# A decoder step on one core: the second feed-forward layer with Strassen products for all eleven pairs of hidden tiles

## The chip, the cores and the metric

The kernel runs as one launch on one core of a Trainium2 chip. The metric is the device time of that launch in microseconds; smaller is better. Engines are named as in the profile: PE multiplies matrices (PEld loads its stationary operands), DVE is the vector engine, ACT the scalar engine, POOL is GpSimd, SP issues the DMAs.

## The reference, cut to what matters

One inference step of a two-layer decoder trunk over 512 prompt rows and 32 sample rows, all in float32. Layer 0 is a half feed-forward, a gMLP mixer, a second half feed-forward and a gated input embedding; layer 1 has an attention mixer instead. The change touches the second feed-forward of layer 0 and the end of the gMLP in front of it:

```python
h = h + 0.5 * swiglu(rmsnorm(h, ffn1_norm[i]), ffn1_w1[i], ffn1_w3[i], ffn1_w2[i])
xn = rmsnorm(h, mix_norm[i])
mix, v_rows = gmlp_mix(xn, ...)           # ends with (u * s) @ w_out
h = h + mix
h = h + 0.5 * swiglu(rmsnorm(h, ffn2_norm[i]), ffn2_w1[i], ffn2_w3[i], ffn2_w2[i])
...
def swiglu(x, w1, w3, w2):
    return (jax.nn.silu(x @ w1) * (x @ w3)) @ w2
```

The model is 1024 wide, the hidden layer 2816 wide.

## The kernel before

**Data.** The residual stream lies transposed in SBUF: eight tiles `h[c]` of 128 rows (channels) and T = 544 columns (tokens). A float32 product is made of three products of rounded parts: an operand x is split into `hi` (ACT, a cast to fp32r) and `lo` = x - hi (DVE), and PE adds hi·hi, hi·lo and lo·hi. So each weight block of 128x1024 costs one load (512 KB, SP), one ACT cast and one DVE subtraction (`_split`) before PE can use it.

**The gMLP's end.** Eight output tiles, one per `c`, 48 matmuls each (`tile_mm`, `mm`: 8 stationary blocks, 3 parts, columns in two pieces of 256 and 288). After each, DVE adds the result to `h[c]` (L667), and `on_chunk(c)` prepares the next norm: `prep` makes the split of g·h (ACT L297 for hi, DVE L298 for lo; g is the norm's gain), `ssq` squares h (ACT L324) and POOL adds the square to the norm's sum (L326). After c = 1, 3 and 5 `forms` builds, for a pair of tiles, the sums of quarters that the Strassen products need (ACT L307, DVE L311 to L314, and two splits, ACT L285 and DVE L286).

**The feed-forward layer.** The 2816 hidden rows are 11 pairs of two 128-row tiles (of `w1` and `w3` at once). Pair 0 is **plain**: four `tile_mm` with the columns in full, whose first also brings the norm's factor: `rstd` splits the sum of squares, sums it over the partitions with four matmuls (L362), and `rsqrt_steps` makes 1/sqrt of it on ACT and DVE. Pairs 1 to 10 are **Strassen** pairs in Winograd's form: the 256 x 1024 block times 1024 x 544 as seven products (`products`, named "1" to "7") of 24 matmuls with 272 columns, into PSUM tiles A, B and C; four of the seven weight operands are sums of blocks that DVE makes (`_sum`, L184), all seven are split. `evict` combines the products in SBUF, `gate` multiplies by rstd, silu and product. Between the products stand the matmuls of the second matrix (`second`).

**What sets the order.** Weights are a stream of `pieces`; `prepare` at piece u splits to u + 2, makes sums to u + 2 (in the layer u + 3) and loads to u + 4 (u + 6), by `self.ahead`. All 128x1024 blocks come from one pool of 45 buffers, so a load waits until an older block is let go. The gMLP is ordered by a scheduler when the program is built; the layer's steps (`ffn_steps`) keep the order of the code on PE, ACT, DVE and POOL. On the chip each engine takes its instructions in that fixed order.

Of the kernel before, what the change touches and what calls it, by code (L numbers as in the profile page):

```python
# [26 lines left out]
ALU = mybir.AluOpType  # L27
# [27 lines left out]
PLAIN = (2, 1, 1, 1)  # L55

SEVEN = "1562734"

# [36 lines left out]
class Builder:  # L95
# [37 lines left out]
    def set_stream(self):  # L133
        self.chain, self.pending, self.bg, self.pages = None, [], [], {}
        self.aps, self.raws = [], {}
        self.pieces, self.sums, self.split = [], {}, {}
# [12 lines left out]
    def seven(self, aps):  # L149
# [5 lines left out]
        for k, x, op, y in (("5", a21, "+", a22), ("6", (r, "5"), "-", a11), ("7", a11, "-", a21),  # L155
                            ("3", a12, "-", (r, "6"))):
            d[k] = dict(key=(r, k), sum=(x, op, y))
        for v in d.values():
            v.update(n=1024)
# [14 lines left out]

    def _sum(self):
        p = self.pieces[self.p_sum]
        self.p_sum += 1
        if p["sum"] is None:
            return
        a, op, b = p["sum"]  # L180
        get = lambda x: self._raw(x, 1024) if isinstance(x[1], int) else self.sums[x]
        a, b = get(a), get(b)
        t = self.flat(1024)
        self.nc.vector.tensor_tensor(t, a, b, ALU.add if op == "+" else ALU.subtract)  # L184
        self.sums[p["key"]] = t
# [184 lines left out]
    def ffn_slots(self, skip=1):  # L370
# [16 lines left out]
    def ffn_pieces(self, n):  # L387
# [4 lines left out]
        for kind, at, k, part in self.ffn_slots(PLAIN[n]):  # L392
            if kind == "g":
                if at not in d:
                    d[at] = self.seven([i["w13"][n, at - 1, x] for x in range(4)])
# [10 lines left out]
    def ffn(self, h, box, gcol, rstd, on_chunk, plain=1):  # L406
# [30 lines left out]
        assert self.chain is None  # L437
        for j, a, g in first:
            todo[a].extend(([None] * 3 if j == 0 else []) + self.gate(hid, rstd, j, a, g))
        with self.tc.manual_schedule(engines={eng.PE, eng.Activation, eng.DVE, eng.Pool}):  # L440
            self.ffn_steps(h, xf, rstd, hid, todo, plain, on_chunk)
# [23 lines left out]
    def ffn_steps(self, h, xf, rstd, hid, todo, plain, on_chunk):  # L465
# [8 lines left out]
        def products(j, k, part):  # L474
            if k == "1" and j not in tiles:
                tiles[j] = {}
            t = tiles[j]
            if k in "152" and "ABC"["125".index(k)] not in t:
                if k == "2":
                    t["B"] = [self.pb()[:, :HT] for _ in range(2)]  # L480
                else:
                    t["A" if k == "1" else "C"] = self.ps()[:, :, :HT]
            out = t["A" if k in "1674" else "C" if k in "53" else "B"]
            dst = out if k == "2" else [out[:, w] for w in range(2)]
            hi, lo = self.take()
            for kp in range(NKP):
                xh, xl = xf[kp][k]
                for n, (a, b) in enumerate(((hi, xh), (hi, xl), (lo, xh))):
                    for w in range(2):
                        c = slice(512 * w + P * kp, 512 * w + P * kp + P)  # L490
                        nc.tensor.matmul(dst[w], a[:, c], b, start=k in "152" and kp == 0 and n == 0,  # L491
# [3 lines left out]
        def evict(j, k):  # L495
            t = tiles[j]
            if k in "156":
                t["r" + k] = q2(self.tmp())
                nc.scalar.copy(t["r" + k], t["C" if k == "5" else "A"])  # L499
                return  # L500
            if k == "2":
                t["g"] = self.big(), self.big()
            g = t["g"]
# [5 lines left out]
            elif k == "3":  # L509
# [1008 lines left out]
```

## Time and profile before

| | before |
|---|---|
| time, median of 3 runs | 2063.28 us (2062.68 to 2063.79) |
| time of the profiled execution | 2064.12 us |
| its span, first to last instruction | 2062.4 us |
| PE busy | 2042.4 us, 99% of the span |
| DVE busy | 1507.2 us, 73% |
| ACT busy | 950.4 us, 46% |
| POOL busy | 184.2 us, 9% |

Busy shares are averages over the whole span. PE's idle time, not its share, tells where something can be won or lost, and it is read stage by stage from the waits and the timeline. The profiled execution's own time lies 1.7 us above its span and 0.84 us above the median.

### The profile page before, as it was taken

What the parts mean: (1) busy time and instruction counts of PE and PEld (TensorE: products, weight loads), DVE (VectorE), ACT (ScalarE), POOL (GpSimd) and SP (SyncE); (2) the same over time, 40 slices, a digit from 0 to 9 for tenths busy, and PEclk for the clock granted to TensorE, in tenths of its full rate; (3) what the DMA queues carried; (4) which work ended last, traced back from release to release, by engine and by line L of the source; (5) the groups of instructions that cost most, each with busy time, mean ns of one, the idle gap of its engine ahead of it and who ended that gap; (6) DMA issues with size and microseconds to landing.
All of it is one profiled execution on the core that took longest, in us unless ns stands there. A gap on an engine that the chain in (4) does not pass through costs nothing.

```text
span 2062.4 us, 38838 instructions
## 1 busy us (share of the span) xinstructions
PE 2042.4 (99%) x16432; PEld 2012.4 (98%) x16432; DVE 1507.2 (73%) x1861; ACT 950.4 (46%) x1421; POOL 184.2 (9%) x222
## 2 busy tenths in 40 slices
PE   8999999999999999999999999999999999999999
PEld 8999999999999999999999999999987999999999
DVE  7877777556687778776688777786476888777773
ACT  7534344423554344454456343534365754344451
POOL 0000000410100000043060000001141200000020
PEclk9999999999999999999999999999999999999999
DMA  5233234212223222432374323314669222222431
GB/s 185 84 110 107 74 109 141 97 44 83 83 92 113 73 105 80 154 99 82 107 255 162 113 85 110 105 69 136 193 204 323 99 99 85 100 103 82 130 97 44
DMA packets 93823, 237.95 MB, mean 115 GB/s; under 512 B 9538, under 2 KB 27490, under 8 KB 93650
## 3 DMA queue, kind: packets, MB, share of 16 engines
q1 hardware_dynamic: 93506, 235.44, 34.1%
q8 instruction: 129, 2.11, 0.4%
q14 instruction: 44, 0.36, 0.1%
q10 hardware_dynamic: 144, 0.04, 0.0%
HBM read 218.95 MB, written 16.49 MB: 114 GB/s over the span
## 4 chain that ended last, share of the span: by engine, by line
PE 92%; DVE 3%; ACT 2%; issue 1%; DMA 1%; POOL 0%; SPq 0%; DVEq 0%; ACTq 0%; POOLq 0%
PE ps L491 33%; PE ps L241 16%; PE ps L247 16%; PE ps L245 16%; PE pb L491 5%; DVE big L199 1%; ACT big L198 1%; PE ps L1272 1%; PE ps L1268 1%; PE ps L1271 1%; ACT big L285 0%; DVE big L184 0%; DVE big L286 0%; PE ps L1223 0%; PE ps L829 0%
## 5 line engine op out<-in xcount | busy, mean ns | idle before, releaser
L491 PE MATMUL ps<-big,big 128*128 128x272 f32 x5616 | 727.7, 288 | 1.8 <-DVE big L508 1.3
L491 PEld LDWEIGHTS ps<-big,big 128*128 128x128 f32 x5616 | 714.2, 188 | 2.4 <-issue 1.6
L199 DVE TENSOR_TENSOR big<-big,big 128x1024 fp32r<-128x1024 f32 (+2 forms) x538 | 591.9, 1103 | 105.5 <-ACT big L198 105.0
L198 ACT CAST big<-big 128x1024 fp32r<-128x1024 f32 (+2 forms) x538 | 488.0, 932 | 267.6 <-DVE big L184 262.8
L241 PE MATMUL ps<-big,big 128*128 128x256 f32 (+1 forms) x2684 | 558.8, 289 | 7.6 <-ACT big L198 7.6
L247 PE MATMUL ps<-big,big 128*128 128x256 f32 x2684 | 554.9, 289 | 1.5 <-DVE big L199 1.5
L245 PE MATMUL ps<-big,big 128*128 128x256 f32 x2684 | 554.0, 287 | 0.0
L241 PEld LDWEIGHTS ps<-big,big 128*128 128x128 f32 x2684 | 430.9, 189 | 11.3 <-ACT big L198 8.5
L247 PEld LDWEIGHTS ps<-big,big 128*128 128x128 f32 x2684 | 429.8, 188 | 3.1 <-DVE big L199 2.7
L245 PEld LDWEIGHTS ps<-big,big 128*128 128x128 f32 x2684 | 432.5, 189 | 0.0
L326 POOL TENSOR_TENSOR st<-st,tmp 128x544 f32<-128x544 f32 (+1 forms) x63 | 87.5, 1388 | 1587.7 <-ACT tmp L324 1587.5
L530 DVE SCALAR_TENSOR_TENSOR big<-ps,big 128x544 f32<-128x544 f32 x160 | 115.6, 723 | 106.5 <-PE ps L247 106.4
L184 DVE TENSOR_TENSOR big<-big,big 128x1024 f32<-128x1024 f32 x156 | 190.2, 1219 | 0.0
L499 ACT COPY tmp<-ps 128x544 f32<-128x544 f32 x117 | 71.7, 613 | 141.2 <-PE ps L491 141.2
L454 ACT ACTIVATE big<-big 128x544 f32<-128x544 f32 x88 | 58.0, 660 | 163.2 <-DVE big L451 162.0
L491 PE MATMUL pb<-big,big 128*128 128x272 f32 x936 | 124.0, 288 | 0.0
L451 DVE TENSOR_TENSOR big<-big,st 128x1088 f32<-128x1088 f32 x88 | 113.4, 1290 | 10.6 <-ACT big L513 8.8
L491 PEld LDWEIGHTS pb<-big,big 128*128 128x128 f32 x936 | 120.2, 188 | 0.0
L286 DVE TENSOR_TENSOR big<-big,big 128x544 fp32r<-128x544 f32 (+1 forms) x112 | 82.1, 739 | 36.4 <-ACT big L285 36.3
L297 ACT ACTIVATE big<-big,gains 128x544 fp32r<-128x544 f32 (+1 forms) x80 | 55.8, 704 | 104.6 <-DVE big L530 64.9
L298 DVE SCALAR_TENSOR_TENSOR big<-big,gains,big 128x544 fp32r<-128x544 f32 (+1 forms) x80 | 65.8, 830 | 25.8 <-ACT big L297 25.8
L285 ACT CAST big<-big 128x544 fp32r<-128x544 f32 (+1 forms) x112 | 71.3, 644 | 17.8 <-DVE big L457 9.0
(208 smaller groups left out, 1430.8 us busy)
## 6 DMA issues: line engine op xcount, KB each, us to landing
big<-in_w SPq DMA_DIRECT2D x156, 512.0 KB
big<-in_w2a SPq DMA_DIRECT2D x64, 512.0 KB
big<-in_w2b SPq DMA_DIRECT2D x32, 384.0 KB
big<-in_w13p SPq DMA_DIRECT2D x16, 512.0 KB
big<-in_win SPq DMA_DIRECT2D x16, 512.0 KB
big<-in_wg SPq DMA_DIRECT2D x16, 512.0 KB
big<-in_ck SPq DMA_DIRECT2D x16, 512.0 KB
big<-in_cv SPq DMA_DIRECT2D x16, 512.0 KB
```

Of the source, the lines that this page charges most:

```text
L184: self.nc.vector.tensor_tensor(t, a, b, ALU.add if op == "+" else ALU.subtract)
L198: self.nc.scalar.copy(hi, src)
L199: self.nc.vector.tensor_tensor(lo, src, hi.bitcast(F32), ALU.subtract)
L241: i = nc.tensor.matmul(out[:, a:b], wh, xh[:, a:b], start=s, stop=False)
L245: nc.tensor.matmul(out[:, a:b], wh, xl[:, a:b], start=False, stop=False)
L247: nc.tensor.matmul(out[:, a:b], wl, xh[:, a:b], start=False, stop=e)
L286: self.nc.vector.tensor_tensor(pair[:, 1, cols], src, pair[:, 0, cols].bitcast(F32), ALU.subtract)
L326: nc.gpsimd.tensor_tensor(acc[:, cols], acc[:, cols], sq, ALU.add)
L451: tt(g, g, rstd.unsqueeze(1).broadcast_to([P, 2, T]), ALU.mult)
L491: nc.tensor.matmul(dst[w], a[:, c], b, start=k in "152" and kp == 0 and n == 0, stop=kp == NKP - 1 and n == 2, skip_group_check=True)
L499: nc.scalar.copy(t["r" + k], t["C" if k == "5" else "A"])
L530: nc.vector.scalar_tensor_tensor(h[c], whole(out), 0.5, h[c], ALU.mult, ALU.add)
```

## The change

The second feed-forward layer has no plain pair any more (`PLAIN[1] = 0`): pair 0 is a Strassen pair too. Its products come in the order "1", "2", "3", "6", "5", "7", and "4" follows behind the first product of pair 1; "3" gets a PSUM tile of its own (D), and `evict` combines in another order. From the third last output tile of the gMLP on, `ahead` is (3, 4, 6), so pair 0's loads, sums and splits begin there, and a sum that needs another makes it on demand (`_operand`). The norm's sum is split before the layer's steps (`rstd_parts`), and the four matmuls and the rsqrt come in front of product "6". The fourth `forms` is made after c = 7. Line numbers shift: L199 is L208 after the change, L184 is L186, L298 is L307, L311 to L314 are L320 to L323, L286 is L295, L358 is L366, L362 is L375, L491 is L513, L667 is L692.

```diff
-PLAIN = (2, 1, 1, 1)
+PLAIN = (2, 0, 1, 1)
+PLAIN_FIRST = "123657"
...
+    def _operand(self, x):
+        if isinstance(x[1], int):
+            return self._raw(x, 1024)
+        if x not in self.sums:
+            a, op, b = self.defs[x]
+            a, b = self._operand(a), self._operand(b)
+            t = self.flat(1024)
+            self.nc.vector.tensor_tensor(t, a, b, ALU.add if op == "+" else ALU.subtract)
+            self.sums[x] = t
+        return self.sums[x]
+
     def _sum(self):
         p = self.pieces[self.p_sum]
         self.p_sum += 1
...
+        if p["sum"]:
+            self._operand(p["key"])
...
-    def rstd(self, acc):
-
+    def rstd_parts(self, acc):
         parts = self.tmp(F32R), self.tmp(F32R)
         self.nc.scalar.copy(parts[0], acc)
         self.nc.vector.tensor_tensor(parts[1], acc, parts[0].bitcast(F32), ALU.subtract)
+        return parts
+
+    def rstd(self, acc, parts=None):
+
+        parts = parts or self.rstd_parts(acc)
         sums = [self.pb()[:, :HT] for _ in range(2)]
...
-            gs = [("g", j, k, None) for k in SEVEN]
+            gs = [("g", j, k, None) for k in (SEVEN if j else PLAIN_FIRST)]
+            if j == 1 and skip == 0:
+                gs.insert(1, ("g", 0, "4", None))
...
+        parts = self.rstd_parts(box["acc"]) if rstd is None else None
...
         def products(j, k, part):
+            nonlocal rstd
+            if rstd is None and k == "6":
+                rstd = self.rstd(None, parts)
...
+            own = "3" if j == 0 else ""
+            fresh = k in "152" + own
...
-            out = t["A" if k in "1674" else "C" if k in "53" else "B"]
+            out = t["A" if k in "1674" else "D" if k in own else "C" if k in "53" else "B"]
...
-            if k in "156":
+            if k in "15" or k == ("6" if j else "3"):
                 t["r" + k] = q2(self.tmp())
-                nc.scalar.copy(t["r" + k], t["C" if k == "5" else "A"])
-                return
+                nc.scalar.copy(t["r" + k], t["C" if k == "5" else "D" if k == "3" else "A"])
+            if j == 0 and k == "6":
+                tt(t["r3"], t["A"], t["r3"], add)
...
-            elif k == "3":
-                tt(g[0][:, :, HT:], t["C"], t["r6"], add)
+            elif k == ("3" if j else "5"):
+                tt(g[0][:, :, HT:], t["C"], t["r6" if j else "r3"], add)
...
         for c in range(NC_):
+            if c == NC_ - 3:
+                self.ahead = (3, 4, 6)
             p = self.tile_mm(m)
...
-        on, nxt = self.next_norm(h, G_FFN2, early={1: 0, 3: 1, 5: 2})
+        on, nxt = self.next_norm(h, G_FFN2, early={1: 0, 3: 1, 5: 2, 7: 3})
...
-        self.ffn(h, box, G_FFN2, None, on)
+        self.ffn(h, box, G_FFN2, None, on, PLAIN[1])
...
-        w13.append(np.stack([_blocks(w1[n][:, 256:]), _blocks(w3[n][:, 256:])], 3).reshape(NPAIR - 1, 4, P, 1024))
+        w13.append(np.stack([_blocks(w1[n]), _blocks(w3[n])], 3).reshape(NPAIR, 4, P, 1024))
```

**DVE at the gMLP's last two output tiles.** Before, from the update of `h[6]` (`big_89`, first row) to the prep of `h[7]`; `big_5922` and `big_5984` are the splits of g·h[6] and g·h[7], the L199 rows are splits of the plain pair's weights:

```order
L667 TENSOR_TENSOR big_89<-ps_5872,big_89 128x544
L286 TENSOR_TENSOR big_5858<-tmp_5856,big_5858 128x544
L199 TENSOR_TENSOR big_5867<-big_5732,big_5866 128x1024
L298 SCALAR_TENSOR_TENSOR big_5922<-big_89,gains,big_5922 128x544
L199 TENSOR_TENSOR big_5929<-big_5794,big_5928 128x1024
L667 TENSOR_TENSOR big_89<-ps_5934,big_89 128x544
L298 SCALAR_TENSOR_TENSOR big_5984<-big_89,gains,big_5984 128x544
```

After the change, from the same update; `big_5872` is the block a12 of pair 0 (the operand of product "2"), the three L186 rows are the sums of "5", "6" and "3", and `big_5934` and `big_5994` are the splits of g·h[6] and g·h[7]:

```order
L692 TENSOR_TENSOR big_89<-ps_5884,big_89 128x544
L295 TENSOR_TENSOR big_5860<-tmp_5858,big_5860 128x544
L692 TENSOR_TENSOR big_89<-ps_5944,big_89 128x544
L208 TENSOR_TENSOR big_5875<-big_5872,big_5874 128x1024
L186 TENSOR_TENSOR big_5878<-big_5868,big_5870 128x1024
L186 TENSOR_TENSOR big_5880<-big_5878,big_5732 128x1024
L186 TENSOR_TENSOR big_5882<-big_5872,big_5880 128x1024
L307 SCALAR_TENSOR_TENSOR big_5934<-big_89,gains,big_5934 128x544
L208 TENSOR_TENSOR big_5941<-big_5882,big_5940 128x1024
L307 SCALAR_TENSOR_TENSOR big_5994<-big_89,gains,big_5994 128x544
```

The split of g·h[6], which stood between the two L667 rows, now stands behind the second one, and behind the split for "2" and the three sums; the split of g·h[7] stands behind the split for "3".

**DVE further on in pair 0.** After the change, from the last row of the fourth `forms`; L366 (one row earlier) was the norm's split, `big_6046`, `big_6078` and `big_6119` are the splits for "6", "5" and "7", L529 reads product "2" out of its two PSUM tiles `pb`, `big_6159` is the first split for pair 1, L352 is the first step of the rsqrt:

```order
L295 TENSOR_TENSOR big_6006<-tmp_6004,big_6006 128x544
L208 TENSOR_TENSOR big_6046<-big_5880,big_6045 128x1024
L208 TENSOR_TENSOR big_6078<-big_5878,big_6077 128x1024
L186 TENSOR_TENSOR big_6081<-big_5732,big_5868 128x1024
L529 TENSOR_TENSOR big_6114<-pb_6049,tmp_6075 128x272
L529 TENSOR_TENSOR big_6114<-pb_6050,tmp_6075 128x272
L208 TENSOR_TENSOR big_6119<-big_6081,big_6118 128x1024
L208 TENSOR_TENSOR big_6159<-big_6083,big_6158 128x1024
L352 SCALAR_TENSOR_TENSOR tmp_6129<-st_6128 128x544
```

Before the change the fourth `forms` stood at the plain pair's end, ACT copied the plain tiles out, and nothing on DVE had to read a `pb` tile ahead of the norm's matmuls; now the two L529 rows do, and stand behind two splits and the sum of "7" (`big_6081`).

**PE where the norm's sum is taken.** Before, in the second tile of the plain pair, whose stationary blocks are `big_5928`; L362 reads the norm's split `tmp_6040` into the tiles `pb`:

```order
L241 MATMUL ps_6075<-big_5570,big_5928 128x256
L241 MATMUL ps_6075<-big_5570,big_5928 128x288
L362 MATMUL pb_6044<-tmp_6040,onesr 128x272
L362 MATMUL pb_6045<-tmp_6040,onesr 128x272
L245 MATMUL ps_6075<-big_5570,big_5928 128x256
```

After the change, behind the last stationary block of product "3" (`ps_6089`) and in front of product "6" (`ps_6020`):

```order
L513 MATMUL ps_6089<-big_5994,big_5940 128x272 x4
L513 MATMUL ps_6089<-big_5994,big_5941 128x272 x2
L375 MATMUL pb_6122<-tmp_6014,onesr 128x272
L375 MATMUL pb_6123<-tmp_6014,onesr 128x272
L375 MATMUL pb_6122<-tmp_6015,onesr 128x272
L375 MATMUL pb_6123<-tmp_6015,onesr 128x272
L513 MATMUL ps_6020<-big_5582,big_6045 128x272 x4
L513 MATMUL ps_6020<-big_5582,big_6046 128x272 x2
```

The four matmuls stood among those of a plain tile, two and two; now they stand together between two products, and take the two `pb` tiles that product "2" has held.

## Rows read from the trace of the kernel before

**Rows 1.** The page's first part: busy time of each engine, its share of the span, and the number of its instructions.

```profile
PE 2042.4 (99%) x16432; PEld 2012.4 (98%) x16432; DVE 1507.2 (73%) x1861; ACT 950.4 (46%) x1421; POOL 184.2 (9%) x222
```

**Rows 2.** Who PE waited for: first over the whole execution (two of its eleven rows: the longest, and the next longest single wait), then from 480 to 620 us, where one wait is all there is. Columns: total us, times, longest us.

```profile
PE ps L241 <- ACT big L198: 7.6, 3, 7.1
...
PE pb L1243 <- DVE tmp L1239: 1.1, 1, 1.1
...
PE ps L491 <- DVE big L508: 0.7, 1, 0.7
```

**Rows 3.** PE's instructions in order of time: start us, length us, engine, line, operation, tiles, count; in brackets the idle time before and what ended it. First the first matmuls of the plain pair, then the norm's four, then the first products of the Strassen pairs.

```profile
540.08 0.41 PE L241 MATMUL ps<-big,big 128*128 128x256 f32 x2
...
547.05 0.41 PE L362 MATMUL pb<-tmp,onesr 128*128 128x272 f32 x2
...
564.48 9.23 PE L491 MATMUL ps<-big,big 128*128 128x272 f32 x72
573.54 3.19 PE L491 MATMUL pb<-big,big 128*128 128x272 f32 x24
576.57 6.19 PE L491 MATMUL ps<-big,big 128*128 128x272 f32 x48
583.48 0.74 PE L491 MATMUL ps<-big,big 128*128 128x272 f32 x4 [0.72 <-DVE big L508]
```

**Rows 4.** DVE's instructions in order of time across the end of the gMLP and the start of the second feed-forward layer, same columns.

```profile
529.87 0.79 DVE L298 SCALAR_TENSOR_TENSOR big<-big,gains,big 128x544 fp32r<-128x544 f32 x1 [0.82 <-ACT big L297]
531.70 0.78 DVE L311 TENSOR_TENSOR tmp<-big 128x544 f32<-128x544 f32 x1 [1.04 <-ACT big L307]
532.51 0.44 DVE L313 TENSOR_TENSOR tmp<-big,tmp 128x272 f32<-128x272 f32 x1
532.99 0.44 DVE L314 TENSOR_TENSOR tmp<-big,tmp 128x272 f32<-128x272 f32 x1
533.35 0.72 DVE L286 TENSOR_TENSOR big<-tmp,big 128x544 fp32r<-128x544 f32 x1
534.30 0.72 DVE L667 TENSOR_TENSOR big<-ps,big 128x544 f32<-128x544 f32 x1 [0.24 <-PE ps L247]
534.94 0.72 DVE L286 TENSOR_TENSOR big<-tmp,big 128x544 fp32r<-128x544 f32 x1
535.58 1.22 DVE L199 TENSOR_TENSOR big<-big,big 128x1024 fp32r<-128x1024 f32 x1
536.71 1.89 DVE L298 SCALAR_TENSOR_TENSOR big<-big,gains,big 128x544 fp32r<-128x544 f32 x1
538.52 1.21 DVE L199 TENSOR_TENSOR big<-big,big 128x1024 fp32r<-128x1024 f32 x1
540.28 0.72 DVE L667 TENSOR_TENSOR big<-ps,big 128x544 f32<-128x544 f32 x1 [0.54 <-PE ps L247]
541.88 0.79 DVE L298 SCALAR_TENSOR_TENSOR big<-big,gains,big 128x544 fp32r<-128x544 f32 x1 [0.88 <-ACT big L297]
543.37 1.61 DVE L199 TENSOR_TENSOR big<-big,big 128x1024 fp32r<-128x1024 f32 x1 [0.70 <-ACT big L198]
...
549.90 0.79 DVE L346 SCALAR_TENSOR_TENSOR tmp<-pb,tmp 128x272 f32<-128x272 f32 x2
550.60 1.22 DVE L199 TENSOR_TENSOR big<-big,big 128x1024 fp32r<-128x1024 f32 x1
551.73 0.72 DVE L347 SCALAR_TENSOR_TENSOR st<-tmp,st 128x544 f32<-128x544 f32 x1
```

**Rows 5.** ACT's instructions after the last tile of the gMLP, same columns.

```profile
541.09 0.75 ACT L297 ACTIVATE big<-big,gains 128x544 fp32r<-128x544 f32 x1 [3.74 <-DVE big L667]
541.75 0.64 ACT L324 ACTIVATE tmp<-big 128x544 f32<-128x544 f32 x1
542.30 1.03 ACT L198 CAST big<-big 128x1024 fp32r<-128x1024 f32 x1
```

**Rows 6.** POOL's last two additions to the norm's sum in the gMLP, same columns.

```profile
535.92 2.09 POOL L326 TENSOR_TENSOR st<-st,tmp 128x544 f32<-128x544 f32 x1 [4.03 <-ACT tmp L324]
542.53 1.36 POOL L326 TENSOR_TENSOR st<-st,tmp 128x544 f32<-128x544 f32 x1 [4.52 <-ACT tmp L324]
```

**Rows 7.** SP's loads around the gMLP's output tiles (start us, length us over the merged issues), and the rate of all DMA from 498 to 520 us in 40 slices of 0.55 us (GB/s).

```profile
510.40 6.30 SPq L165 DMA_DIRECT2D big<-in_w13p  x2
...
GB/s 0 0 0 0 0 82 320 410 142 0 0 0 0 0 0 0 0 0 0 0 0 0 0 30 119 127 387 291 45 0 0 0 0 0 0 141 246 372 194 0
```

**Rows 8.** PE at the start of the program: the first matmul and the idle time before it, matmul pairs at 11.71 and at 13.48 us, and the windows from 8 to 10 and 14 to 16 us (busy us and count of PE, PEld, DVE, ACT, POOL, granted clock, DMA share, GB/s).

```profile
7.12 0.82 PE L241 MATMUL ps<-big,big 128*128 128x256 f32 x2 [7.12 <-ACT big L198]
...
11.71 0.66 PE L241 MATMUL ps<-big,big 128*128 128x256 f32 x2
12.17 0.66 PE L245 MATMUL ps<-big,big 128*128 128x256 f32 x2
...
13.48 0.41 PE L245 MATMUL ps<-big,big 128*128 128x256 f32 x2
13.73 0.42 PE L247 MATMUL ps<-big,big 128*128 128x256 f32 x2
...
8.00:10.00 2.00, 2.00 (x9) 1.69 (x9) 1.99 (x4) 1.41 (x3) 0.00 (x0) 1.00 1.03 402
14.00:16.00 2.00, 2.00 (x19) 2.00 (x18) 1.90 (x3) 2.00 (x5) 0.00 (x0) 1.00 0.61 229
```

More of the change, by code (lines that the diff above doesn't have):

```diff
@@ L135, in set_stream @@
         self.aps, self.raws = [], {}
-        self.pieces, self.sums, self.split = [], {}, {}
+        self.pieces, self.sums, self.split, self.defs = [], {}, {}, {}
         self.p_next = self.p_split = self.p_sum = self.a_load = 0
@@ L157, in seven @@
             d[k] = dict(key=(r, k), sum=(x, op, y))
+            self.defs[r, k] = x, op, y
         for v in d.values():
@@ L177, in _sum @@
         self.p_sum += 1
-        if p["sum"] is None:
-            return
[L180 to L185, printed above, removed]
+        if p["sum"]:
+            self._operand(p["key"])
     def _split(self):
@@ L394, in ffn_pieces @@
                 if at not in d:
-                    d[at] = self.seven([i["w13"][n, at - 1, x] for x in range(4)])
+                    d[at] = self.seven([i["w13"][n, at, x] for x in range(4)])
                 self.pieces.append(d[at][k])
@@ L440, in ffn @@
         with self.tc.manual_schedule(engines={eng.PE, eng.Activation, eng.DVE, eng.Pool}):
-            self.ffn_steps(h, xf, rstd, hid, todo, plain, on_chunk)
+            self.ffn_steps(h, xf, rstd, hid, todo, plain, on_chunk, parts)
         self.ahead = (2, 2, 4)
@@ L463, in gate, with ffn_steps @@
         return [one, two, three, four]
-    def ffn_steps(self, h, xf, rstd, hid, todo, plain, on_chunk):
+    def ffn_steps(self, h, xf, rstd, hid, todo, plain, on_chunk, parts):
         nc = self.nc
@@ L477, in products @@
             t = tiles[j]
-            if k in "152" and "ABC"["125".index(k)] not in t:
+            own = "3" if j == 0 else ""
+            fresh = k in "152" + own
+            if fresh:
                 if k == "2":
@@ L481, in products @@
                 else:
-                    t["A" if k == "1" else "C"] = self.ps()[:, :, :HT]
-            out = t["A" if k in "1674" else "C" if k in "53" else "B"]
+                    t["A" if k == "1" else "C" if k == "5" else "D"] = self.ps()[:, :, :HT]
+            out = t["A" if k in "1674" else "D" if k in own else "C" if k in "53" else "B"]
             dst = out if k == "2" else [out[:, w] for w in range(2)]
@@ L490, in products @@
                         c = slice(512 * w + P * kp, 512 * w + P * kp + P)
-                        nc.tensor.matmul(dst[w], a[:, c], b, start=k in "152" and kp == 0 and n == 0,
+                        nc.tensor.matmul(dst[w], a[:, c], b, start=fresh and kp == 0 and n == 0,
                                          stop=kp == NKP - 1 and n == 2, skip_group_check=True)
@@ L496, in evict @@
             t = tiles[j]
-            if k in "156":
+            if k in "15" or k == ("6" if j else "3"):
                 t["r" + k] = q2(self.tmp())
-                nc.scalar.copy(t["r" + k], t["C" if k == "5" else "A"])
-                return
+                nc.scalar.copy(t["r" + k], t["C" if k == "5" else "D" if k == "3" else "A"])
+            if j == 0 and k == "6":
+                tt(t["r3"], t["A"], t["r3"], add)
             if k == "2":
                 t["g"] = self.big(), self.big()
-            g = t["g"]
+            g = t.get("g")
             if k == "2":
@@ L508, in evict @@
                 tt(g[1][:, :, HT:], t["A"], t["r5"], add)
-            elif k == "3":
-                tt(g[0][:, :, HT:], t["C"], t["r6"], add)
+            elif k == ("3" if j else "5"):
+                tt(g[0][:, :, HT:], t["C"], t["r6" if j else "r3"], add)
                 todo[0].extend(self.gate(hid, rstd, j, 0, g[0]))
-            else:
+            elif k == "4":
                 nc.scalar.copy(g[1][:, :, :HT], t["A"])
```

## The prediction

> **What bounds the kernel now.** First the page's busy times: PE is busy 2042.4 of 2062.4 us [rows 1], so a change is worth what it takes from PE's matmuls and what it puts into or takes from PE's waits. Then PE's waits: the longest is 7.1 us at the program's start, the next longest single one 1.1, and from 480 to 620 us, where the change lies, PE waits once, 0.7 us, for DVE's L508 [rows 2]. Then PE's timeline there: the plain pair's first matmul starts at 540.08, the first Strassen product at 564.48, so the plain pair takes 24.40 us without a gap [rows 3]. DVE has room on average, but across this stretch its timeline shows what it must do between the gMLP's last tile and the layer, and in which order [rows 4]. DVE takes its rows in the order in which they stand, so I set the order after the change against the durations of before.
>
> **Matmuls.** Three products (72 matmuls) take 564.48 to 573.54, 9.06 us, and the fourth 573.54 to 576.57 [rows 3]: 3.02 us per product. Seven are 21.1 us; the norm's four matmuls, as wide as a product's (the first two at 547.05), add 4 x 0.126 = 0.5. Against 24.40: **-2.8 us**.
>
> **More work off PE.** Seven splits instead of four and four sums: seven DVE operations of 128x1024 more, at 1.13 us from start to start (550.60 to 551.73 [rows 4]), 8 us, and three ACT casts at 1.03 [rows 5]. Were they spread over the gMLP's last three tiles they would be hidden. So the question is where they stand, and that the order rows in the section on the change show.
>
> **Stall A, in product "1".** Behind the update of h[6] DVE has one more row, then the update of h[7], which waits for the gMLP's last matmul. Before, DVE did two weight splits and the split of g·h[6] in that time (535.58 to 539.7 [rows 4]); after, it has nothing to do there but wait, since split "2", three sums and the split of g·h[6] all stand behind. The data are not late: the loads are let go by blocks that DVE and PE finish by about 513 (the last by the split that follows 511), and the load issued at 510.40 shows its burst in the slices from 510.7 to 513.4 [rows 7], so the last is there by about 517. SP issues as many loads as before, four blocks of pair 0 in the place of four plain ones, and POOL's queue gets nothing; pair 1's loads are let go by matmuls of the gMLP's last tile and read by DVE only from about 559, so they are no term. From the update's start at 540.28 [rows 4]:
> update 0.64 (its step to the next independent row, 534.30 to 534.94), 540.92; split "2" 1.13, 542.05; sums "5" and "6", each waiting for the one before, 1.22 + 0.05 (the gap from L313 to L314 is 0.03), 543.32 and 544.59; sum "3" 1.13, 545.72; split of g·h[6] 0.79, 546.51.
> Product "1" needs that split for its 21st matmul: 540.08 + 20 x 0.126 = 542.6. ACT's hi of g·h[6] now stands behind the square of h[7] and comes at 541.0 + 0.64 + 0.75 = 542.4 [rows 5], just in time. So PE waits **3.9 us**. POOL's addition of that square starts about 541.8 and falls on the first sum. In the trace such a meeting stretched a DVE operation from 0.79 to 1.89 (536.71 against 541.88, POOL from 535.92) and another from 1.23 to 1.61 (543.37, POOL from 542.53) [rows 4, 6]. The bounds are 0 and 1.1 us; the first case is nearer (POOL comes while DVE is busy and takes its turn), so I take **+1.1**. Products "2" and "3" find their operands in time.
>
> **Stall B, before product "6".** The norm's four matmuls write the two tiles that "2" holds, so they wait for both L529 rows. DVE's chain goes on from 545.72 (without POOL's 1.1, which shifts both stalls' ends alike): split "3" waits for sum "3" and its cast (1.07 from cast start to split start, 542.30 to 543.37 [rows 4, 5]), 546.95; split of g·h[7] 548.1; the fourth forms 549.05 to 552.7 (1.65 to its first L286 by 531.70 to 533.35, then three rows at 0.63, the norm's split among them); split "6" to 554.0; split "5", held by its cast behind ACT's copy of "1", from 554.45; sum "7" 555.6; L529 twice from 556.7 to 557.5 (0.70 for two of 272 columns, 549.90 to 550.60, and its own tail). PE arrives at 546.5 + 0.5 + 2 x 3.02 = 553.05 and waits for the second half until 557.4, some of it behind the first: **4.2 us**; 3.6 without the two cast waits, 4.6 if ACT slips further.
>
> **Stall C, "7" and "4".** With the norm at 557.5, "6" ends near 561.0 and "5" near 564.0. "7" goes into the tile that DVE must have read after "6"; that row stands behind two splits and the rsqrt (0.76 + 0.70 + 0.72, as 549.14 to 552.4 before), and ends near 564.7. "4" needs the readout of "7", behind two splits, two sums and a gate: near 571.9 against PE at 570.7. That is 0.7 + 1.2. The one wait of this kind in the trace is 0.7 [rows 2], so 0.7 is the low bound and 2.0 the high one; I take **1.5**. That one, at 583.48, I take off, **-0.7**: DVE comes to pair 1 without that queue behind it. If it stays, 0.
>
> **Sum.** -2.8 + 3.9 + 1.1 + 4.2 + 1.5 - 0.7 = **+7.2 us**. The profiled execution took 2064.12, its span and 1.7 around it, so it would take 2071.3; the median of before is 0.84 lower, and so is my forecast for the median: **2070.5**. The lowest bounds give -2.8 + 3.9 + 0 + 3.6 + 0.7 - 0.7 = +4.7 (2068.0), the highest -2.8 + 3.9 + 1.1 + 4.6 + 2.0 - 0 = +8.8 (2072.1).
>
> **Rivals.** (1) **The clock falls.** At the program's start, after 7.1 us of idle, pairs of matmuls (544 columns) start 0.46 us apart until about 13 us, then 0.25 apart: the lower level, 1.2 GHz, then 2.4, though the column of the granted clock says 1.00 in both windows [rows 8]. A stall could do the same here. Six microseconds at half speed are 3 us lost. After A they would be taken out of B, where PE waits 4.2 anyway, and the end would not move; after B they would cover C, and cost 3.0 - 1.5: 2072.0. Against it: the trace has no wait between 1.1 and 7.1 us [rows 2] that shows it either way. Chance 0.2. The Trainium skill has this as a rule (TensorE: Matmul & The Clock Gate, Part 1): the array's clock drops to half when PE has been idle for a while and returns only after sustained work, and the trace agrees at the program's start; by the row alone the sum is +7.2, with the rule holding after B +8.7.
> (2) **The stalls are partly covered**: DVE's operations come closer together, POOL does not get in the way, and B shrinks to about 2. Then -2.8 + 3.9 + 2 + 0.7 - 0.7 = +3.1, 2066.4. It decides if L529 is done by about 555.3. Speaking against: the chain has 12 DVE rows behind A and hardly a gap. Chance 0.1, half of it within 0.2%.
> (3) **Faster.** The operations of DVE are done before the update of h[7], in the 5 us of idle that PE's last tile leaves; then A is gone, B begins 5 us earlier and is gone too, C stays small: -2.8 to -1.5, 2060.5 to 2061.8. It decides if the split of g·h[6] is there by 542.6. The order puts it behind the update, so this needs the instructions to run otherwise than they stand. Chance 0.04.
> (4) **No effect**: pair 0 is worth 2.8 us of PE and the stalls happen to be worth as much; within 0.2%, 0.06.
>
> **How the numbers follow.** A measurement of this kernel can tell about 0.2% (4.1 us) from no change. The likeliest case (0.6) gives 2070.5; with rival 1 the slower side by over 0.2% (above 2067.4) holds 0.85, with half of rival 2; within 0.2% 0.11; faster 0.04. The range leaves out rival 3 and the low half of rival 2 and goes above the highest bound for the clock: 2066.8 to 2073.0.
>
> **What would show it.** Right: after about 542.6 PE waits some 4 to 5 us in the first Strassen product for the split of g·h[6] (L307), DVE idle before the update of h[7] from about 536 to 540; a second wait of about 4 us of the norm's matmuls (L375) for L529; one or two of about 1 us behind; 24 matmuls fewer. PE pairs at 0.46 us behind a stall would show rival 1. Wrong: no wait at L513 near 542, or DVE busy on weights from 536 to 540; then the loads or the order are not what I read.

## The result, and the profile after

The changed kernel takes **2069.9 us** (median of 7 runs, 2069.03 to 2070.89) against 2063.3 for the kernel before on the same chip (7 runs): a ratio of 1.0031, 95% interval 1.0021 to 1.0040, so +6.6 us. The profiled execution took 2069.03 with a span of 2067.2 (before: 2064.12 and 2062.4).

In the changed file the lines have moved: L513 holds the products' matmuls, L375 the norm's, L307 the split of a normalized tile, L208 and L207 a weight's split and its cast, L186 the sums, L529, L523 and L531 the read-outs of "2", "6" and "7", L692 the update of h.

The page's first part, as [rows 1]: 24 matmuls fewer, PE busy 0.9 us less, DVE 10.6 us more, and the span 4.8 us longer.

```profile
PE 2041.5 (99%) x16408; PEld 2010.8 (97%) x16408; DVE 1517.8 (73%) x1873; ACT 953.2 (46%) x1424; POOL 186.1 (9%) x222
```

PE's waits from 480 to 640 us, which answer to the last of [rows 2] (total us, times, longest). The single wait of before, 0.7 us for L508, is gone, and four others stand there, 6.9 us together.

```profile
PE ps L513 <- DVE big L307: 4.7, 1, 4.7
PE ps L513 <- DVE big L531: 0.9, 1, 0.9
PE pb L375 <- DVE big L529: 0.8, 1, 0.8
PE ps L513 <- DVE tmp L523: 0.5, 1, 0.5
```

PE's timeline, as [rows 3] (start us, length us, instruction, count, in brackets the idle time before and what ended it). The first matmul of pair 0 starts at 539.62; product "2" of pair 2, which started at 595.57 before, now starts at 602.08.

```profile
539.62 2.89 PE L513 MATMUL ps<-big,big 128*128 128x272 f32 x20
547.23 1.27 PE L513 MATMUL ps<-big,big 128*128 128x272 f32 x4 [4.73 <-DVE big L307]
548.30 5.35 PE L513 MATMUL pb<-big,big 128*128 128x272 f32 x24
553.49 3.15 PE L513 MATMUL ps<-big,big 128*128 128x272 f32 x24
557.43 0.90 PE L375 MATMUL pb<-tmp,onesr 128*128 128x272 f32 x4 [0.79 <-DVE big L529]
558.16 6.16 PE L513 MATMUL ps<-big,big 128*128 128x272 f32 x48
564.81 6.26 PE L513 MATMUL ps<-big,big 128*128 128x272 f32 x48 [0.48 <-DVE tmp L523]
571.94 9.26 PE L513 MATMUL ps<-big,big 128*128 128x272 f32 x72 [0.87 <-DVE big L531]
...
602.08 3.16 PE L513 MATMUL pb<-big,big 128*128 128x272 f32 x24
```

This stretch, from the first matmul of the second feed-forward layer to product "2" of pair 2, is the measure used for every run below: 595.57 - 540.08 = 55.5 us before, 62.5 after, **+7.0**. What lies behind it differs from one profile to another in no relation to the edits (it takes between 1465.1 and 1467.4 us in all the profiles here, 1466.8 before and 1465.1 in the change); with that, and 0.5 us less ahead of it, the span moved by only 4.8. The row to notice is the third: product "2", 24 matmuls, took 548.30 to 553.49, 5.19 us, where a product takes 3.02 [rows 3]. The windows say why (busy us and count of PE, PEld, DVE, ACT, POOL, then the granted clock, DMA share, GB/s):

```profile
541.00:547.00 6.00, 1.51 (x11) 1.11 (x9) 5.93 (x5) 1.37 (x3) 1.44 (x1) 0.95 0.39 142
547.00:553.00 6.00, 5.77 (x25) 5.77 (x26) 5.45 (x9) 5.15 (x9) 0.00 (x0) 0.50 0.28 90
553.00:559.00 6.00, 5.21 (x40) 4.92 (x39) 5.35 (x7) 3.35 (x7) 0.00 (x0) 0.99 0.00 0
```

From 547 to 553, right behind the wait of 4.7 us, the granted clock is 0.50, that is 1.2 GHz; in the next window it is back. Read in windows of half a microsecond, it fell while PE still stood, at about 546.4, and rose at about 553.2.

DVE's timeline, as [rows 4]. DVE stands idle for 4.43 us ahead of the last update of h; then come a split, the three sums, and only then the split of g·h[6] that PE waits for.

```profile
534.67 0.72 DVE L295 TENSOR_TENSOR big<-tmp,big 128x544 fp32r<-128x544 f32 x1
539.82 0.72 DVE L692 TENSOR_TENSOR big<-ps,big 128x544 f32<-128x544 f32 x1 [4.43 <-PE ps L256]
540.46 1.22 DVE L208 TENSOR_TENSOR big<-big,big 128x1024 fp32r<-128x1024 f32 x1
541.59 4.89 DVE L186 TENSOR_TENSOR big<-big,big 128x1024 f32<-128x1024 f32 x3
546.40 0.78 DVE L307 SCALAR_TENSOR_TENSOR big<-big,gains,big 128x544 fp32r<-128x544 f32 x1
...
556.85 0.78 DVE L529 TENSOR_TENSOR big<-pb,tmp 128x272 f32<-128x272 f32 x2
```

POOL's addition of the square, as [rows 6], runs beside the first of the three sums:

```profile
541.44 1.44 POOL L335 TENSOR_TENSOR st<-st,tmp 128x544 f32<-128x544 f32 x1 [4.42 <-ACT tmp L333]
```

### The profile page after: what moved, and what is told of

It is laid out like the page before. It is cut to its first block, busy times and chain, and to the rows that moved or that the text cites. A ratio compares the mean times of both kernels' runs of the same rounds, so it can differ in the third digit from the quotient of the medians.

```text
span 2067.2 us, 38812 instructions
## 1 busy us (share of the span) xinstructions
PE 2041.5 (99%) x16408; PEld 2010.8 (97%) x16408; DVE 1517.8 (73%) x1873; ACT 953.2 (46%) x1424; POOL 186.1 (9%) x222
## 4 chain that ended last, share of the span: by engine, by line
PE 90%; DVE 4%; ACT 2%; issue 1%; DMA 1%; SPq 0%; POOL 0%; ACTq 0%; DVEq 0%; POOLq 0%
PE ps L513 33%; PE ps L250 15%; PE ps L256 15%; PE ps L254 15%; PE pb L513 6%; DVE big L208 1%; ACT big L207 1%; DVE big L186 1%; PE ps L1297 1%; PE ps L1293 1%; PE ps L1296 1%; DVE big L295 0%; ACT big L294 0%; PE ps L1248 0%; PE ps L854 0%
## 5 line engine op out<-in xcount | busy, mean ns | idle before, releaser
L513 PE MATMUL ps<-big,big 128*128 128x272 f32 x5760 | 747.2, 288 | 7.1 <-DVE big L307 4.7
L513 PEld LDWEIGHTS ps<-big,big 128*128 128x128 f32 x5760 | 732.9, 188 | 8.3 <-DVE big L307 4.9
L208 DVE TENSOR_TENSOR big<-big,big 128x1024 fp32r<-128x1024 f32 (+2 forms) x541 | 594.6, 1102 | 98.5 <-ACT big L207 98.0
L207 ACT CAST big<-big 128x1024 fp32r<-128x1024 f32 (+2 forms) x541 | 490.9, 932 | 275.4 <-DVE big L186 270.2
L250 PE MATMUL ps<-big,big 128*128 128x256 f32 (+1 forms) x2620 | 544.8, 289 | 7.5 <-ACT big L207 7.5
L256 PE MATMUL ps<-big,big 128*128 128x256 f32 (+1 forms) x2620 | 541.1, 288 | 1.4 <-DVE big L208 1.4
L254 PE MATMUL ps<-big,big 128*128 128x256 f32 (+1 forms) x2620 | 540.3, 287 | 0.0
L250 PEld LDWEIGHTS ps<-big,big 128*128 128x128 f32 x2620 | 419.8, 189 | 10.9 <-ACT big L207 8.1
L256 PEld LDWEIGHTS ps<-big,big 128*128 128x128 f32 x2620 | 419.1, 188 | 3.1 <-DVE big L208 2.6
L186 DVE TENSOR_TENSOR big<-big,big 128x1024 f32<-128x1024 f32 x160 | 196.0, 1225 | 0.1
L521 ACT COPY tmp<-ps 128x544 f32<-128x544 f32 x120 | 73.5, 613 | 147.8 <-PE ps L513 147.8
L513 PE MATMUL pb<-big,big 128*128 128x272 f32 x960 | 129.3, 291 | 0.0
L513 PEld LDWEIGHTS pb<-big,big 128*128 128x128 f32 x960 | 125.5, 192 | 0.0
L295 DVE TENSOR_TENSOR big<-big,big 128x544 fp32r<-128x544 f32 (+1 forms) x112 | 82.2, 738 | 37.3 <-ACT big L294 37.1
L307 DVE SCALAR_TENSOR_TENSOR big<-big,gains,big 128x544 fp32r<-128x544 f32 (+1 forms) x80 | 64.6, 815 | 25.5 <-ACT big L306 25.5
L294 ACT CAST big<-big 128x544 fp32r<-128x544 f32 (+1 forms) x112 | 71.4, 644 | 17.9 <-DVE big L473 9.2
```

Of the source, the lines that this page charges most:

```text
L207: self.nc.scalar.copy(hi, src)
L208: self.nc.vector.tensor_tensor(lo, src, hi.bitcast(F32), ALU.subtract)
L250: i = nc.tensor.matmul(out[:, a:b], wh, xh[:, a:b], start=s, stop=False)
L254: nc.tensor.matmul(out[:, a:b], wh, xl[:, a:b], start=False, stop=False)
L256: nc.tensor.matmul(out[:, a:b], wl, xh[:, a:b], start=False, stop=e)
L295: self.nc.vector.tensor_tensor(pair[:, 1, cols], src, pair[:, 0, cols].bitcast(F32), ALU.subtract)
```

## The experiments

Ten kernels were run in three groups, each group on one Trainium2 chip beside the kernel before (2063.38, 2063.01 and 2063.14 us). The theory: the seven products save PE the 2.8 us as reckoned, and DVE's backlog behind the gMLP's last tile costs more than that, wherever PE meets it. The rivals: the sums' place alone, the order alone, the clock, or something in the pair itself.

**Run 1: everything but the pair.** The plain pair 0 is back; early forms, look-ahead and the moved norm operands stay.

```
-PLAIN = (2, 0, 1, 1)
+PLAIN = (2, 1, 1, 1)
```

> The change with its plain pair kept: the look-ahead in the gMLP's last three tiles and the fourth forms after c = 7 stay. My theory: the price of the change is seven more DVE operations of 128x1024 between the gMLP's last matmul and the norm, and they are gone here; no wait above 1 us from 480 to 620 us, at best the 0.7 us for L508 goes too: 2062.5 to 2063.3. Rival, that the look-ahead, its earlier loads or the early forms cost the time: 2066 or more.

Measured: 2062.7 us (11 runs), ratio 0.9994, interval 0.9985 to 1.0003. PE has no wait at all from 480 to 640 us, and the stretch from the first Strassen product to "2" of pair 2 takes 30.13 us (564.29 to 594.42) and not 31.09: L508's 0.7 goes with something that stays in this run (look-ahead, early forms or the moved norm operands, which it does not separate), not with the pair. The whole loss needs the seven-product pair 0 at this place.

**Run 2: PE kept busy through stall A.** 38 matmuls whose result nobody uses, inside product "1", ahead of the matmul that waits. They are added work.

```
 for n, (a, b) in enumerate(((hi, xh), (hi, xl), (lo, xh))):
+    if parts is not None and (j, k, kp, n) == (0, "1", 3, 1):
+        fill = self.pb()[:, :HT]
+        for _ in range(38):
+            nc.tensor.matmul(fill, self.onesr, xf[0]["1"][0], start=True, stop=True)
     for w in range(2):
```

> The change, with 38 matmuls of no use (about 4.8 us) that PE does in the first stall, so that it doesn't idle there. After that stall the profile shows the clock at half. My theory: the end is set by DVE's chain up to L529, and the half clock only fills time in which PE would have waited. So the clock stays at 1.00, the wait of the norm's matmuls grows from 0.8 to about 4 us, and the time stays: 2069.9, give or take 0.7. Rival, that the half clock itself costs about 3 us: 2067.

Measured: 2070.61 us (7 runs), ratio 1.0031, interval 1.0020 to 1.0042, the same as the change; the stretch is 62.8 us (541.55 to 604.34). PE's timeline (L514 is the fill, L517 the products, L533 the read-out of "2"):

```profile
544.28 4.85 PE L514 MATMUL pb<-big,onesr 128*128 128x272 f32 x38
549.17 0.78 PE L517 MATMUL ps<-big,big 128*128 128x272 f32 x4
549.79 3.18 PE L517 MATMUL pb<-big,big 128*128 128x272 f32 x24
552.80 3.17 PE L517 MATMUL ps<-big,big 128*128 128x272 f32 x24
559.38 1.30 PE L375 MATMUL pb<-tmp,onesr 128*128 128x272 f32 x4 [3.40 <-DVE big L533]
560.48 13.09 PE L517 MATMUL ps<-big,big 128*128 128x272 f32 x96
```

The windows of the same stretch, columns as above:

```profile
547.00:553.00 6.00, 5.96 (x48) 5.74 (x47) 5.41 (x8) 3.64 (x6) 0.00 (x0) 1.00 0.00 0
553.00:559.00 6.00, 2.98 (x24) 2.75 (x22) 5.78 (x8) 3.57 (x6) 0.00 (x0) 1.00 0.28 87
559.00:565.00 6.00, 5.62 (x34) 5.65 (x35) 3.93 (x6) 4.23 (x6) 0.00 (x0) 0.72 0.01 1
```

Without the idle stretch the clock stays at 1.00, product "2" takes 3.0 us again, PE comes to the norm 2.6 us sooner after product "1", and waits 3.40 there where it waited 0.79. From the end of stall A to the norm it is 10.2 us in both (549.17 to 559.38 here, 547.23 to 557.43 in the change). So the half clock of the change took its time out of stall B and did not move the end. Now the clock falls in B (0.72 as the mean of that window): the norm's four matmuls took 1.1 us and not 0.5, and the 96 matmuls behind them a row of 13.1, where such a row takes 12.25 at full clock (run 4). Of stall C's two waits, 1.35 us in the change, 0.63 is left.

**Run 3: the sums earlier.** The look-ahead rises at tile 3, to three splits, six sums and eight loads.

```
-            if c == NC_ - 3:
-                self.ahead = (3, 4, 6)
+            if c == 3:
+                self.ahead = (3, 6, 8)
```

> The change, with the look-ahead set at the fourth output tile (c = 3) to (3, 6, 8) in place of (3, 4, 6) at the sixth: the three sums are made two tiles earlier. My theory: the first stall (4.7 us, L307) goes and so the clock stays up; DVE's chain behind the last tile is shorter by a split, three sums and POOL's 1.1, 5.9 us, of which the second stall, now without a slow clock to hide in, keeps about 3 us. Sum -2.8 + 3.0 + 1.4 - 0.7 = +0.9: 2064.2. Rival, that the place of the sums doesn't matter because the second stall takes up what the first gives: 2069 to 2070.

Measured: 2065.98 us (11 runs), ratio 1.0011, interval 1.0002 to 1.0020; stretch 59.1. PE's waits:

```profile
PE pb L375 <- DVE big L529: 2.8, 1, 2.8
PE pb L513 <- DVE big L307: 0.9, 1, 0.9
PE ps L513 <- DVE big L307: 0.7, 1, 0.7
PE ps L513 <- DVE big L531: 0.4, 1, 0.4
```

The 4.7 us fell to 0.7 and 0.9, so the split for "2" and the three sums, which stood between the last update and the split of g·h[6] and now stand ahead of that update, were stall A. The expectation of 2064.2 was missed by 1.8 us: it had neither those two rests nor the clock, which fell to 0.72 behind the 2.8 us at the norm (96 matmuls in 13.3 us).

**Run 4: the sums earlier, the norm and "4" later.** On top of run 3, the norm's matmuls stand ahead of "5", and "4" of pair 0 goes two places further back in pair 1.

```
-                gs.insert(1, ("g", 0, "4", None))
+                gs.insert(3, ("g", 0, "4", None))
-            if rstd is None and k == "6":
+            if rstd is None and k == "5":
```

> The same early sums, the norm's four matmuls in front of product 5 instead of 6, and product 4 of pair 0 two products later (third place in pair 1). My theory: the second stall goes as well, and of the small waits behind some 1.5 us are left: -2.8 + 1.5 - 0.7 = -2.0, 2061.3, faster than both. Rival, that DVE is the bound in pairs 0 and 1 whatever the order: the waits only move to the readouts (L523, L531), 2064 or more.

Measured: 2063.32 us (11 runs), ratio 0.9999, interval 0.9990 to 1.0009; stretch 55.2, clock 1.00 throughout. The loss is gone, the gain is not there, and the time is 2.0 above what was expected: waits of 0.9, 0.7 and 0.2 remain, and weight loads wait a little as well (PEld 0.4 for ACT's L521, 0.2 for L208, 0.5 for nothing that the profile shows).

**Run 5: the sums spread from tile 1.** Run 4 with two steps of look-ahead, so that nothing is left for the last tile.

```
-            if c == 3:
-                self.ahead = (3, 6, 8)
+            if c == 1:
+                self.ahead = (2, 9, 9)
+            if c == 4:
+                self.ahead = (3, 8, 9)
```

> The eight-tile output loop raises the look-ahead twice, at c == 1 to (2, 9, 9) and at c == 4 to (3, 8, 9), so that the five sums and the splits are spread over six tiles and not three; the norm's matmuls stand ahead of product 5, and product 4 two places later in pair 1. Theory (the stalls come from the amount of DVE work between the last tile's start and the norm, and the change's seven-product pair itself saves matmuls): no wait of TensorE over 0.5 us from 530 to 600, clock 1.00, first pair-0 matmul to pair 2's product 2 within 52.5 to 53.5 us (before 55.49), total 2060.5 to 2061.8, below the kernel before. Rival (a seven-product pair at this place always costs DVE as much as it saves TensorE, so the wait only moves into the output tiles, where the sums then delay a tile's eviction): a new wait of 1 us or more in the tiles c = 1 to 5 and a total of 2063 to 2065, as with the sums from tile 3.

Measured: 2070.92 us (5 runs), ratio 1.0039, interval 1.0025 to 1.0053. Both expectations missed the size, the rival had the place. ACT in the gMLP's output tiles, the cast of a norm's half:

```profile
518.54 0.65 ACT L294 CAST big<-tmp 128x544 fp32r<-128x544 f32 x1 [11.83 <-DVE tmp L320]
```

DVE in the same tiles, from the first sums to L320:

```profile
509.93 2.48 DVE L186 TENSOR_TENSOR big<-big,big 128x1024 f32<-128x1024 f32 x2
515.26 0.72 DVE L694 TENSOR_TENSOR big<-ps,big 128x544 f32<-128x544 f32 x1 [2.86 <-PE ps L256]
515.90 1.22 DVE L186 TENSOR_TENSOR big<-big,big 128x1024 f32<-128x1024 f32 x1
517.03 0.78 DVE L307 SCALAR_TENSOR_TENSOR big<-big,gains,big 128x544 fp32r<-128x544 f32 x1
517.73 0.72 DVE L320 TENSOR_TENSOR tmp<-big 128x544 f32<-128x544 f32 x1
```

PE's first matmul of the next tile:

```profile
521.82 0.82 PE L250 MATMUL ps<-big,big 128*128 128x256 f32 x2 [6.60 <-ACT big L207]
```

The weight's cast (L207, at 520.73) stands on ACT behind L294, L294 waits for DVE's L320, L320 stands behind the update L694, and L694 waits for PE's own tile. PE stood 6.6 us for a cast that could start only when PE had finished the tile before; from 520 to 525 us the granted clock was 0.50, and it was back only at about 529.5. With the second wait, 1.1 us, pair 0 began 10 us later than before (550.07 against 540.08). Behind that, the run shows what the pair is worth alone: with no wait left, the stretch took 51.7 us (550.07 to 601.73).

**Run 6: no look-ahead.**

```
-            if c == NC_ - 3:
-                self.ahead = (3, 4, 6)
```

> The changed kernel without the line that raises the look-ahead in the output loop: pair 0 still has seven products, and their sums and splits are made as late as in the other pairs. Theory (DVE's work ahead of the norm is what TensorE waits for, whichever instruction carries it; the look-ahead only chooses where the wait stands): the stall of 4.7 us ahead of product 1 goes, and one of 5 to 7 us comes at products 3 or 6 or at the norm, total 2068.5 to 2071.5. Rival (the sums crowded into the last three tiles are the whole cause): without them no wait over 1 us and a total of 2062 to 2065.

Measured: 2071.06 us (5 runs), ratio 1.0035, interval 1.0022 to 1.0048; stretch 62.3. Stall A is gone, and product "3" waits for its cast, which waits for the sums. PE's waits from 440 to 640 us:

```profile
PE ps L513 <- ACT big L207: 5.8, 1, 5.8
PE ps L513 <- DVE big L531: 0.9, 1, 0.9
PE ps L513 <- DVE tmp L523: 0.4, 1, 0.4
```

The three sums cost about the same ahead of "3" as ahead of "1".

**Run 7: only the norm later.**

```
-            if rstd is None and k == "6":
+            if rstd is None and k == "5":
```

> The changed kernel with the norm's matmuls one product later, ahead of product 5 and not of 6. Theory (one backlog of DVE, met at whichever instruction needs it first): the 0.8 us at the norm goes, the wait for product 1 stays at 4.7, and the later ones (products 7 and 4 of the next steps) grow to 2 to 4 us, total 2068.3 to 2069.8. Rival (each wait is its own cost, and can be taken out alone): the 0.8 goes and nothing grows, total 2067.5 to 2068.2 or lower if the clock's fall has nothing left to hide in: then the norm's place is where the slow clock's 2.8 us were paid and the end moves by them.

Measured: 2070.64 us (5 runs), ratio 1.0036, interval 1.0023 to 1.0050; stretch 61.6. The time is 0.8 above what was expected and that of the change; the waits went as expected: 0.8 and 0.5 gone, the last one up from 0.9 to 2.3. PE's waits:

```profile
PE ps L513 <- DVE big L307: 4.7, 1, 4.7
PE ps L513 <- DVE big L531: 2.3, 1, 2.3
```

**Run 8: DVE and ACT of the last two tiles in written order.**

```
+        with self.tc.manual_schedule(engines={eng.Activation, eng.DVE}):
+            for c in range(6, NC_):
+                out_tile(c)
```

> The changed kernel with the instructions of VectorE and ScalarE of the last two output tiles kept in the order in which they are written (tile's residual addition and norm first, then sums and splits). Theory (the amount of DVE work between the last tile and the norm decides, the order only which wait is longest): the first wait (product 1) stays within 4 to 6 us or moves to the norm, total 2069 to 2073. Rival (the scheduler's order, which puts three sums ahead of the first split, is the cause): the wait for product 1 falls under 1.5 us with no other over 2, total 2064 to 2066.

Measured: 2071.99 us (4 runs), ratio 1.0041, interval 1.0026 to 1.0056; stretch 62.9. This order is no better: product "1" waits no more, "2" waits 1.0, and the norm's matmuls the rest. But it does not clear the order as such. DVE makes the three sums in its idle time here (536.14 to 539.88), so their data were there; yet the update of h[6] now stands behind them (539.80, not 534.04), and that of h[7] comes at 544.35 and not at 539.82. An order with the update and the split of h[6] first and the sums in the idle time behind them was not run. The two longest waits:

```profile
PE pb L375 <- DVE big L529: 6.8, 1, 6.8
PE pb L513 <- ACT big L306: 0.7, 1, 0.7
```

**Run 9: one sum in each tile from 3 to 6**, the norm and "4" as in run 4; **run 10: the same sums, the norm and "4" as in the change.**

```
-            if c == NC_ - 3:
+            if c == 4:
                 self.ahead = (3, 4, 6)
+            k = {3: '5', 4: '6', 5: '3', 6: '7'}.get(c)
+            if k:
+                self._operand(next(p for p in self.pieces[self.p_next:] if p["key"][1] == k)["key"])
```

> One sum in each of the output tiles c = 3, 4, 5 and 6 (those of products 5, 6, 3 and 7, in this order; the look-ahead for splits rises at c == 4), the norm's matmuls ahead of product 5, product 4 two places later in pair 1. No tile then has to carry three sums, as the tile c = 4 had with the sums from tile 3, or two ahead of its successor's split, as with two steps of look-ahead. Theory (what counts is DVE's work between the start of a tile and the split that the next but one needs): no wait of TensorE over 0.6 us between 500 and 600, clock 1.00 throughout, first pair-0 matmul to pair 2's product 2 within 53 to 54 us (before 55.49), total 2061.0 to 2062.2, some 0.05 to 0.1 per cent below the kernel before. Rival (DVE has no room at all in these tiles, its pauses there belong to its own waits): a wait of 1 us or more in a tile c = 3 to 7 and 2063 or more.

> The sums spread as in the run with one in each tile, but the norm's matmuls stay ahead of product 6 and product 4 where the change has it. Theory (the backlog of DVE ahead of product 1 was the first wait, the norm's chain the second): the 4.7 us ahead of product 1 is gone, 1.5 to 3 us stand at the norm, 0.5 to 1.5 each at the two waits for A's bank after it, the clock falls for part of a stretch or not at all, total 2063.5 to 2065.5. Rival (the sums alone are the whole loss): no wait over 1 us, 2061 to 2062.5, as the run with all three edits.

Measured: run 9 2063.41 us (11 runs), ratio 1.0002, interval 0.9993 to 1.0011; stretch 54.1. Run 10 2065.76 (11 runs), ratio 1.0012, interval 1.0003 to 1.0021; stretch 57.8. PE's waits in run 9 from 440 to 640 us:

```profile
PE ps L256 <- DVE big L208: 0.8, 1, 0.8
PE ps L513 <- DVE big L307: 0.8, 1, 0.8
PE ps L513 <- DVE big L531: 0.3, 1, 0.3
```

And in run 10:

```profile
PE pb L375 <- DVE big L529: 2.7, 1, 2.7
PE ps L256 <- DVE big L208: 0.8, 1, 0.8
PE ps L513 <- DVE big L307: 0.8, 1, 0.8
```

Run 9 shortened the stretch by 1.4 us against before and paid 0.8 of it in an output tile ahead of it (L256); its median misses the expected 2061.0 to 2062.2. Run 10 came 0.3 above its window (2063.5 to 2065.5) and had none of the waits expected behind the norm; the wait at the norm itself, 1.5 to 3 us, came as expected. With the sums spread, the norm's chain is the next wait, and behind its 2.7 us the clock fell again (0.72 from 553 to 559). No version beat the kernel before: runs 1, 4 and 9 are level with it within their intervals.

## Why the prediction was right, step by step

The forecast was 2070.5 (2066.8 to 2073.0), the result 2069.9. In the stretch the sum was +7.2 and the trace shows +7.0; the terms below are off by 0.3 us at most, in both directions, and part of the closeness is that these errors cancel. The profiled execution was forecast at 2071.3 and took 2069.03, since the parts outside the stretch were 2.2 us shorter in it.

- **Matmuls, -2.8: right.** Run 5 has the seven-product stretch without a wait, 51.7 us. Run 1 has the plain one without a wait: 24.40 for the plain pair [rows 3] plus 30.13 is 54.5. The difference is -2.9.
- **Stall A, 3.9 + 1.1: right, cause and size.** The wait was 4.73; the 20 matmuls in front took 2.88 from start to start of the wait, 0.36 more than 20 x 0.126. DVE stood idle before the update, from 535.4 to 539.8, as the order rows had it. POOL's meeting with the first sum came: three sums took 4.81 (541.59 to 546.40) where 3.7 was reckoned. The value was an estimate between 0 and 1.1, and the upper end was it.
- **Stall B, 4.2: the size right, its form not.** PE waited only 0.79. So the second wait of about 4 us, which the prediction named as a sign of being right, did not appear, and the sign of rival 1 did. The rest went into the half clock: the tail of "1" took 1.07 and not 0.50, product "2" 5.19 and not 3.02, together 2.7 us, and about 0.4 more at the edges of the stops ("3" and the norm, 0.13 and 0.23 over). That is rival 1 in its "after A" case, as it was worked out: taken out of B, the end not moved. It had been given a chance of 0.2, and the fall came at the first stall. Run 2 shows that the end did not hang on it. DVE's chain behind the split of g·h[6] was a little shorter than reckoned: 10.2 us from the end of A's wait to the end of B's (547.23 to 557.43), not 10.9 (546.5 to 557.4).
- **Stall C, 1.5: right.** Waits of 0.48 and 0.87 where 0.7 and 1.2 had been reckoned, and 0.35 at the restarts, which no term had: 1.7. The 1.5 was a value between two bounds, so that it came this near is partly luck.
- **L508's wait, -0.7: the number right, the reason not tested by the change alone.** It vanishes in run 1 too, where pair 0 is plain, so it is the look-ahead, the earlier forms or the moved norm operands that take DVE's queue away; no run separates them.
- **Rival 2** (partly covered, 2066.4) did not come about here; runs 3 and 10 reach its time (2066.0 and 2065.8) by another road, with stall A nearly gone and 2.7 to 2.8 us left at the norm. **Rival 3** (faster) would have needed the sums ahead of the last update with the updates in their place; run 8 has the first without the second, and run 9 puts them into earlier tiles and gets level, where one of those tiles already waits 0.8 us for DVE.

What the ten runs say together: each wait can be taken away, and DVE's work then meets PE one step later (A to "3" in run 6, B to "4" in run 7, A to B in run 8) or in an earlier output tile (run 5). The totals of these four and of run 2 lie between 2070.6 and 2072.0. With seven products in pair 0 the total came down only where the sums went into the tiles from 3 on (2066.0 in run 3, 2065.8 in run 10), and to the level of before only where the norm and "4" came later as well (runs 4 and 9). The gain of the seven products is not seen in a time: in run 9 the trace has 1.4 us less in the stretch and 0.8 more in an output tile, and the 0.6 between them is less than the interval of the measurement shows.

## What to carry to other kernels

Where the faster matmul form needs more operands from another engine, reckon that engine's rows between the last tile of the layer before and the first instruction that needs its results, in their order: the average of 73% busy said there was room, and the 4.4 us of idle that DVE had lay ahead of an update behind which, in the order as built, the sums stood. Here moving the waiting instruction moved the wait; spreading the work over earlier tiles removed most of it, as long as no tile's own cast came to stand behind it. And a stall of a few microseconds also slowed the matmuls behind it: that cost nothing where a longer wait for DVE followed (the change against run 2), and some 2 us where none did (run 10, whose norm and next 168 matmuls took 23.7 us from start to start and not 21.6).

## What the runs showed of the hardware

**The clock falls inside a kernel, behind a single wait.** Read in windows of half a microsecond, the granted clock is 1.00 or 0.50 (1.2 GHz), with other values only where it changes; 0.72 in the longer windows above is a mean over both. It went to 0.50 in each kernel here in which PE stood for 2.7 us or more inside the stretch or in an output tile ahead of it (the change and runs 2, 3, 5, 6, 7, 8 and 10), and stayed at 1.00 behind the 2.3 us of run 7 and behind the waits of 0.9 us and less in runs 4 and 9. It fell while PE still stood, or, behind the 2.8 and 2.7 us of runs 3 and 10, just after PE had resumed. The price was 2.7 us behind the wait of 4.7, and 1.4 and 1.6 behind those of 3.4 and 2.8 (runs 2 and 3: the norm's four matmuls 1.1 us and not 0.5, the row of 96 behind them 13.1 and 13.3 and not 12.25). The Trainium skill (TensorE: Matmul & The Clock Gate, Part 1) has the array's clock halved after idle time and back after sustained work; the traces agree, with 0.50 behind the stall and 0.99 in the window after it.

**POOL's addition can cost DVE nearly its own length.** The same sum (L186, 128x1024) in run 9, with POOL's addition of 128x544 beside the first of these and none beside the second:

```profile
525.24 2.39 DVE L186 TENSOR_TENSOR big<-big,big 128x1024 f32<-128x1024 f32 x1
...
532.90 1.21 DVE L186 TENSOR_TENSOR big<-big,big 128x1024 f32<-128x1024 f32 x1
```

POOL's addition beside the first of them:

```profile
525.17 1.37 POOL L335 TENSOR_TENSOR st<-st,tmp 128x544 f32<-128x544 f32 x1 [6.38 <-ACT tmp L333]
```

1.2 us more, near POOL's 1.37. The one that pays need not be the operation that runs when POOL starts: in the same run POOL's addition of 538.11 lasted 3.44 us, the sum at 538.47 beside it took 1.22, and the split at 540.27 took 2.36, where the next one, at 543.89, took 1.22. And it need not be the full length: the split at 543.37 [rows 4], which met an addition already under way since 542.53 [rows 6], took 1.61. The Trainium skill (GPSIMD Engine Reference, section 8) says that GpSimd shares its SBUF interfaces with VectorE and contends with instructions that have two SBUF inputs, as these have; the trace agrees and gives the price.

**A stop of PE costs more than the wait shown**, in the length of the rows before and behind it: in the change 0.36 us ahead of stall A, 0.36 on the two sides of stall B, and 0.35 around the two stops of stall C together. A part of this is that the profile counts a row to the end of its last matmul: 20 matmuls at steps of 0.126 us have a row of 2.67 in run 9.
